# The first product of a chunked recurrent scan as one whole-array matmul for two heads instead of two half-array matmuls

## The chip, the core and the metric

The kernel runs on one core of one Trainium2 chip. A core has a matrix engine (TensorE, PE in the profile, with its weight loader PEld), a vector engine (DVE), a scalar engine (ACT), GpSimd (POOL) and a queue engine for transfers (SP). The metric is the device time of one execution in microseconds (us).

## What is computed

One block of a streaming encoder on an input of 2048 frames by 1024 channels, all in float32: a normalisation, one wide input projection, two branches, gates, an output projection, a residual and a last normalisation. The change touches the first branch, a recurrence per head (16 heads of 64 channels):

```python
def frame_step(S, inp):
    r_t, w_t, k_t, v_t, a_t, b_t = inp
    sa = jnp.einsum('bhij,bhj->bhi', S, a_t)
    S = S * w_t[:, :, None, :] + sa[..., None] * b_t[:, :, None, :] + v_t[..., None] * k_t[:, :, None, :]
    return S, jnp.einsum('bhij,bhj->bhi', S, r_t)
...
h = rms_norm(x, norm_g[l])
z = h @ w_in[l]
zs, gate_a, u, gate_b, m_a, m_b = jnp.split(z, SPLIT_POINTS, axis=-1)
...
merged = jax.nn.sigmoid(m_a) * (y_a @ p_a[l]) + jax.nn.sigmoid(m_b) * (y_b @ p_b[l])
x = x + merged @ w_out[l]
```

The second branch is a diagonal complex state-space scan (S5). The kernel does not walk frame by frame: it takes chunks of 64 frames, solves a triangular system for each chunk, and carries the 64 by 64 state of each head from chunk to chunk.

## The kernel before

**Work units.** Frames are cut into four blocks of 512 (`tb`), heads into eight pairs (`p`); a unit is a pair of heads in one block of frames, 32 in all. Each of them goes through `prep1` (elementwise work), `prep2` (products inside each chunk, the triangular solve on DVE in `solve`), `scan` and two post steps. Three units are in work at a time: while `scan` runs for one, `prep2` runs for the next and `prep1` for the one after.

**The scan.** A unit has eight chunks, so there are 256 chunks in all. Both heads of a pair lie side by side on the 128 partitions: head 0 on partitions 0 to 63, head 1 on 64 to 127 (`HS`). Of each chunk `cur` is a 128 by 128 array (tile SU): its diagonal 64 by 64 blocks hold the two heads' states, the others the chunk's values. A chunk has three slots:

- slot 1: px, the first product, with AT as weights and `cur` as the moving operand, one matmul for each head (L928); DVE copies px from PSUM (the matrix engine's output memory) to rh; ACT makes us, the decayed state (L933).
- slot 2: po gets the state's part of the output (L937); pu is the product of the solved inverse R with rh (L940); DVE and ACT scale it back into `cur` (L941, L942).
- slot 3: pn is the product that makes the next state (L946); DVE writes the next chunk's state (L954); po gets its second part (L956).

px, pn and the second part of po use 128 rows and 64 columns of the array, po's first part and pu 64 by 64.

**AT** is filled in `prep2`: products A of L819 are masked or scaled into it (L825 to L827), a piece of it goes out by DMA for the triangular solve (L832), and L906 writes its diagonal blocks at the end.

**What sets the order.** The order is written out by hand: the loop at the end of the function calls, slot by slot, one step of `scan`, one of `prep2` and so on, and then takes one or two pieces of the projections from a stream (`gm`), six matmuls of 512 columns each (L488 to L490, operands split in two parts of the type fp32r, three products). So on PE, small products of the scan stand between projection pieces. DVE's small chain of the solve is woven in by the class `Woven`, whose helper line is L75: most DVE instructions carry that line in the profile.

After the scan (about 2170 us) come the S5 branch and the output stage, which the change does not touch.

Of the kernel before, what the change touches and what calls it, by code (L numbers as in the profile page):

```python
# [10 lines left out]
F32 = mybir.dt.float32  # L11
F32R = mybir.dt.float32r
AF = mybir.ActivationFunctionType
ALU = mybir.AluOpType
# [3 lines left out]
P = 128  # L18
# [5 lines left out]
C = 64  # L24
NC = TB // C
# [28 lines left out]


class Woven:
    """An engine whose every call is followed by one call of a chain of small dependent ones."""

    def __init__(self, eng):
        self.eng, self.chain, self.due = eng, iter(()), 0  # L60
# [21 lines left out]
def tile_rwkv7_s5_block(  # L82
# [32 lines left out]
    pe, act, pool, sp = nc.tensor, nc.scalar, nc.gpsimd, nc.sync  # L115
    raw_dve = nc.vector
    dve = Woven(raw_dve)
    x = x[0]
    out = out[0]
# [26 lines left out]
    ones = wp.tile([P, 4, P], F32, tag="raw", name="ones")[:, 0, :]  # L146
# [6 lines left out]
    for i in range(2):  # L153
        for j in range(2):
            pool.affine_select(
                out=amask[64 * i:64 * i + 64, j, :], in_=amask[64 * i:64 * i + 64, j, :],
# [107 lines left out]
    if True:  # L264
        one = ph1.enter_context(tc.tile_pool(name="one", bufs=1))
        phu = ExitStack()
        u1 = phu.enter_context(tc.tile_pool(name="u1", bufs=1, side="right"))
        sm = ph1.enter_context(tc.tile_pool(name="sm", bufs=3))
# [7 lines left out]
        up = phup.enter_context(tc.tile_pool(name="up", bufs=2))  # L276
        ust = up.tile([P, NP, C], F32, tag="ust", bufs=1, name="ust")
        pool.memset(ust, 0.0)
        HS = (slice(0, 64), slice(64, 128))
# [526 lines left out]
        am = amask.rearrange("p a t -> p (a t)").unsqueeze(1)  # L806

        def prep2(p, tb):
            n = f"_{p}_{tb}"
            u = U[p, tb]  # L810
            bk, ar, v, dd = u["bk"], u["ar"], u["v"], u["dd"]
            at = up.tile([P, NC, 2, 2 * C], F32, tag="AT", name="AT" + n)
            ld = drx.tile([2, 2, NC, 32, 32], F32, tag="ld", name="ld" + n)
            for c2 in range(NC // 4):
                pas = [psm.tile([P, 4, 2 * C], F32, tag="m", name=f"A{n}_{c2}_{h}") for h in range(2)]
                for i in range(4):
                    c = 4 * c2 + i
                    for h in range(2):
                        pe.matmul(pas[h][:, i, :], bk[HS[h], c, h:h + 2, :].rearrange("p a s -> p (a s)"), ar[HS[h], c, :], start=True, stop=True)  # L819
                cs_ = slice(4 * c2, 4 * c2 + 4)  # L820
                for h in range(2):
                    o_ = HS[1 - h]
                    for i in range(4):
                        c = 4 * c2 + i
                        act.activation(out=at[HS[h], c, h, 0:C], in_=pas[h][HS[h], i, 0:C], func=AF.Copy, scale=dd[HS[h], c:c + 1])  # L825
                    dve.tensor_tensor(out=at[o_, cs_, h, 0:C], in0=pas[h][o_, :, 0:C], in1=am[o_, :, 0:C].to_broadcast([C, 4, C]), op=ALU.mult)
                    dve.tensor_tensor(out=at[:, cs_, h, C:2 * C], in0=pas[h][:, :, C:2 * C], in1=am[:, :, C:2 * C].to_broadcast([P, 4, C]), op=ALU.mult)  # L827
                if c2 == 1:
                    for h in range(2):
                        for b in range(2):  # L830
                            s0 = 64 * h + 32 * b
                            sp.dma_start(out=ld[h, b].rearrange("c s t -> s c t"), in_=at[s0:s0 + 32, :, h, 32 * b:32 * b + 32])  # L832
                yield
            ix = u1.tile([P, 32, 32], F32, tag="IX", name="IX" + n)
            ldf = ld.rearrange("h b c s t -> (h b c) s t")
# [47 lines left out]
            r64 = up.tile([P, NC, C], F32, tag="R64", name="R64" + n)  # L883
            for h in range(2):
                for b in range(2):
                    s0 = 64 * h + 32 * b
# [5 lines left out]
            t11 = u1.tile([P, NC, 32], F32, tag="TM", name="T11" + n)  # L892
# [4 lines left out]
            pz = psm.tile([P, TB], F32, tag="m", name="pz" + n)  # L897
            for c in range(NC):
                for h in range(2):
                    s0 = 64 * h  # L900
                    pe.matmul(pz[s0 + 32:s0 + 64, 32 * c:32 * c + 32], at[s0:s0 + 32, c, h, 32:64], t11[s0:s0 + 32, c, :], start=True, stop=True)
            for h in range(2):
                s0 = 64 * h + 32
                act.copy(zt[s0:s0 + 32].rearrange("p c t -> p (c t)"), pz[s0:s0 + 32, 0:256])
            for h in range(2):
                act.copy(at[HS[h], :, h, 0:C], ar[HS[h], :, 0:C])  # L906
            yield
            pr = psm.tile([P, TB], F32, tag="m", name="pr" + n)
            for c in range(NC):
                for h in range(2):  # L910
                    s0 = 64 * h
                    pe.matmul(pr[s0:s0 + 32, 32 * c:32 * c + 32], zt[s0 + 32:s0 + 64, c, :], r64[s0 + 32:s0 + 64, c, 32:64], start=True, stop=True)
            for h in range(2):
                s0 = 64 * h
# [3 lines left out]
        def scan(p, tb):  # L918
            n = f"_{p}_{tb}"
            u = U[p, tb]  # L920
            ar, at, r64, bt, decs, dd, su = (u[k] for k in ("ar", "at", "r64", "bt", "dec", "dd", "su"))
            po = u["po"] = pso.tile([P, TB], F32, tag="o", name="po" + n)
            for c in range(NC):
                dec = decs[:, c, :]
                cur = su[:, c, :]
                px = pst.tile([P, 512], F32, tag="st", name=f"px{n}_{c}")
                for h in range(2):
                    pe.matmul(px[HS[h], 0:C], at[:, c, h, 0:C], cur[:, HS[h]], start=True, stop=True)  # L928
                rh = sm.tile([P, C], F32, tag="rh", name=f"rh{n}_{c}")
                dve.tensor_copy(rh, px[:, 0:C])  # L930
                us = sm.tile([P, C], F32, tag="us", name=f"us{n}_{c}")
                for h in range(2):
                    act.activation(out=us[HS[h]], in_=cur[HS[h], HS[h]], func=AF.Copy, scale=dec[HS[h]])  # L933
                yield
                oc = po[:, c * C:(c + 1) * C]
                for h in range(2):
                    pe.matmul(oc[HS[h]], cur[HS[h], HS[h]], ar[HS[h], c, C:2 * C], start=True, stop=False)  # L937
                pu = pst.tile([P, 512], F32, tag="st", name=f"pu{n}_{c}")
                for h in range(2):
                    pe.matmul(pu[HS[h], 0:C], r64[HS[h], c, :], rh[HS[h]], start=True, stop=True)  # L940
                dve.tensor_scalar(out=cur[0:64, 0:64], in0=pu[0:64, 0:C], scalar1=dd[0:64, c:c + 1], scalar2=None, op0=ALU.mult)  # L941
                act.activation(out=cur[64:128, 64:128], in_=pu[64:128, 0:C], func=AF.Copy, scale=dd[64:128, c:c + 1])  # L942
                yield
                pn = pst.tile([P, 512], F32, tag="st", name=f"pn{n}_{c}")
                for h in range(2):
                    pe.matmul(pn[HS[h], 0:C], bt[:, c, h, :], cur[:, HS[h]], start=True, stop=True)  # L946
                for h in range(2):
                    if c + 1 < NC:
                        nxt = su[HS[h], c + 1, HS[h]]
                    elif tb % 2 == 0:  # L950
                        nxt = U[p, tb + 1]["su"][HS[h], 0, HS[h]]
                    else:
                        nxt = ust[HS[h], p, :]
                    (raw_dve if h == 0 else dve).scalar_tensor_tensor(out=nxt, in0=pn[HS[h], 0:C], scalar=dec[HS[h]], in1=us[HS[h]], op0=ALU.mult, op1=ALU.add)  # L954
                for h in range(2):
                    pe.matmul(oc[HS[h]], cur[:, HS[h]], at[:, c, h, C:2 * C], start=False, stop=True)  # L956
                yield

        MU, AD, SU = ALU.mult, ALU.add, ALU.subtract
# [543 lines left out]
        with tc.manual_schedule():  # L1503
# [13 lines left out]
            for n in range(-1, NU + 1):  # L1517
                credit = OFF if n == 0 else credit if n > NU - 2 else 0.0
                sc = scan(*units[n]) if 0 <= n < NU else none
                p2 = prep2(*units[n + 1]) if n + 1 < NU else none  # L1520
                a = units[n + 2] if n + 2 < NU else None
                b = units[n - 1] if 1 <= n else None
# [73 lines left out]
    if True:  # L1596
# [3 lines left out]
        for tb in range(NTB):  # L1600
# [44 lines left out]
            for j in range(TB // P):  # L1645
# [16 lines left out]
                for q in range(2):  # L1662
                    qs = slice(q * 512, (q + 1) * 512)
                    dve.scalar_tensor_tensor(out=sq[:, qs], in0=xt[:, qs], scalar=ss[:, 0:1], in1=fgb[:, qs], op0=ALU.mult, op1=ALU.mult)
                    if tb == NTB - 1 and j == TB // P - 1 or q:
                        o_ = qs if tb == NTB - 1 and j == TB // P - 1 else slice(0, D)
# [31 lines left out]
```

## Time and profile before

| what | value |
|---|---|
| median of 3 runs | 2781.81 us (2778.14 to 2783.49) |
| profiled execution, span from its first to its last instruction | 2782.6 us |
| mean granted TensorE clock | 0.988 |
| PE, PEld busy | 2690.9 us (97%), 1959.3 us (70%) |
| DVE, ACT, POOL busy | 1898.7 us (68%), 1372.9 us (49%), 611.4 us (22%) |
| px (L928), records on PE | 1024, from 147.0 to 2166.6 us |

For the profiled execution there is no time of its own besides its span; the span lies inside the range of the three runs. In the profile a plain f32 product appears as two passes, each with a weight load and a matmul, so the 512 px products are 1024 records. Ends of matmuls are modelled and they overlap: what a matmul costs its engine is read from the distance of starts, not from its duration.

### The profile page before, as it was taken

What the parts mean: (1) busy time and instruction counts of PE and PEld (TensorE: products, weight loads), DVE (VectorE), ACT (ScalarE), POOL (GpSimd) and SP (SyncE); (2) the same over time, 40 slices, a digit from 0 to 9 for tenths busy, and PEclk for the clock granted to TensorE, in tenths of its full rate; (3) what the DMA queues carried; (4) which work ended last, traced back from release to release, by engine and by line L of the source; (5) the groups of instructions that cost most, each with busy time, mean ns of one, the idle gap of its engine ahead of it and who ended that gap; (6) DMA issues with size and microseconds to landing.
All of it is one profiled execution on the core that took longest, in us unless ns stands there. A gap on an engine that the chain in (4) does not pass through costs nothing.

```text
span 2782.6 us, 52007 instructions
## 1 busy us (share of the span) xinstructions
PE 2690.9 (97%) x18700; PEld 1959.3 (70%) x18700; DVE 1898.7 (68%) x5620; ACT 1372.9 (49%) x3355; POOL 611.4 (22%) x985
## 2 busy tenths in 40 slices
PE   6999999999999999999999999999989999999998
PEld 4777677667777766777677777776766777777777
DVE  5656667767666787667776766667668788756544
ACT  6455554555555576555454555555554443423321
POOL 2221212122221333222212121222232200111110
PEclk9999999999999999999999999999989999999999
DMA  3222323222222443323323232322366656756533
GB/s 109 77 77 68 94 76 96 73 82 79 77 84 73 132 126 106 95 77 81 86 69 92 72 89 73 91 81 76 106 177 188 214 141 168 227 181 178 163 113 99
DMA packets 256361, 303.73 MB, mean 109 GB/s; under 512 B 159745, under 2 KB 172134, under 8 KB 255078
## 3 DMA queue, kind: packets, MB, share of 16 engines
q1 hardware_dynamic: 210502, 150.94, 20.3%
q0 software_dynamic: 45600, 149.46, 18.1%
q8 instruction: 148, 2.42, 0.4%
q14 instruction: 111, 0.91, 0.1%
HBM read 219.91 MB, written 71.70 MB: 105 GB/s over the span
## 4 chain that ended last, share of the span: by engine, by line
PE 47%; DVE 6%; DMA 4%; ACT 2%; issue 2%; SPq 0%; POOL 0%; DVEq 0%; POOLq 0%; ACTq 0%
PE pout L1656 2%; PE pout L1658 2%; PE pout L1657 2%; PE pma L488 1%; PE pga L488 1%; PE pmb L488 1%; PE px L928 1%; PE pv L488 1%; PE pk L488 1%; PE pr L488 1%; PE pn L946 1%; PE A L819 1%; PE po L937 1%; DMA sgb<-sb_d 1%; PE pma L490 1%
## 5 line engine op out<-in xcount | busy, mean ns | idle before, releaser
L942 ACT ACTIVATE SU<-pu,dd 64x64 f32<-64x64 f32 x256 | 79.2, 310 | 398.8 <-DVE SU L75 327.6
L869 DVE TENSOR_TENSOR RF<-RF,TM 128x60 f32<-128x60 f32 (+24 forms) x992 | 228.2, 230 | 28.3
L865 DVE TENSOR_TENSOR TM<-RF,IX 128x60 f32<-128x60 f32 (+24 forms) x992 | 227.4, 229 | 26.6 <-DMA IX<-ld 4.3
L933 ACT ACTIVATE us<-SU,dec 64x64 f32<-64x64 f32 x512 | 176.3, 344 | 70.4 <-DVE SU L954 62.8
L75 DVE TENSOR_TENSOR AT<-A,amask 64x256 f32<-64x256 f32 (+1 forms) x256 | 102.2, 418 | 115.9 <-ACT AT L825 110.4
L75 DVE TENSOR_SCALAR SU<-pu,dd 64x64 f32<-64x64 f32 x256 | 70.0, 274 | 162.8 <-PE pu L940 160.3
L954 DVE SCALAR_TENSOR_TENSOR SU<-pn,dec,us 64x64 f32<-64x64 f32 x240 | 65.6, 273 | 110.6 <-PE pn L946 110.1
L825 ACT ACTIVATE AT<-A,dd 64x64 f32<-64x64 f32 x512 | 116.8, 303 | 38.3 <-PE A L819 36.3
L928 PEld LDWEIGHTS px<-SU,AT 128*64 128x64 f32 x1024 | 53.9, 135 | 101.8 <-issue 50.8
L946 PEld LDWEIGHTS pn<-SU,BT 128*64 128x64 f32 x1024 | 54.3, 135 | 98.3 <-issue 40.5
L937 PEld LDWEIGHTS po<-AR,SU 64*64 64x64 f32 x1024 | 50.1, 132 | 97.0 <-issue 88.0
L488 PE MATMUL ppa<-yhi,whi_pa 128*128 128x512 f32 x256 | 115.7, 452 | 2.0 <-ACT whi_pa L224 1.1
L75 DVE COPY rh<-px 128x64 f32<-128x64 f32 x256 | 56.7, 222 | 82.0 <-PE px L928 77.2
L488 PE MATMUL pma<-hhi,whi_ma 128*128 128x512 f32 x256 | 112.7, 440 | 0.0
L488 PE MATMUL pmb<-hhi,whi_mb 128*128 128x512 f32 x256 | 112.6, 440 | 0.0
L488 PE MATMUL pk<-hhi,whi_k 128*128 128x512 f32 x256 | 112.5, 440 | 0.0
L488 PE MATMUL pga<-hhi,whi_ga 128*128 128x512 f32 x256 | 112.2, 438 | 0.0
L488 PE MATMUL pv<-hhi,whi_v 128*128 128x512 f32 x256 | 111.2, 434 | 0.3 <-ACT carry L441 0.3
L488 PE MATMUL pr<-hhi,whi_r 128*128 128x512 f32 x256 | 111.5, 435 | 0.0
L490 PE MATMUL ppa<-yhi,wlo_pa 128*128 128x512 f32 x256 | 103.9, 406 | 2.5 <-DVE wlo_pa L75 2.5
L489 PE MATMUL ppa<-ylo,whi_pa 128*128 128x512 f32 x256 | 103.5, 404 | 0.5 <-DVE ylo L75 0.5
L1656 PE MATMUL pout<-wohi,mhi 128*128 128x512 f32 x256 | 100.5, 392 | 2.9 <-ACT mhi L255 2.8
(373 smaller groups left out, 7942.5 us busy)
## 6 DMA issues: line engine op xcount, KB each, us to landing
IX<-ld SPq DMA_DIRECT2D x128, 128.0 KB
raw_pa<-in_p_a_dram POOLq DMA_DIRECT2D x64, 256.0 KB, 4.6
raw_mb<-in_w_in_dram POOLq DMA_DIRECT2D x50, 256.0 KB, 3.5
raw_r<-in_w_in_dram POOLq DMA_DIRECT2D x36, 256.0 KB, 3.7
raw_k<-in_w_in_dram POOLq DMA_DIRECT2D x36, 256.0 KB, 3.5
raw_v<-in_w_in_dram POOLq DMA_DIRECT2D x36, 256.0 KB, 3.4
raw_ga<-in_w_in_dram POOLq DMA_DIRECT2D x34, 256.0 KB, 3.5
ce<-cw SPq DMA_DIRECT2D x16, 514.0 KB
```

The costliest lines, as they stand in the source:

```text
L75: r = f(*a, **kw)
L488: pe.matmul(ps, hi[:, k, :], xhi[:, kk_, :], start=(kk_ == 0), stop=False)
L489: pe.matmul(ps, hi[:, k, :], xlo[:, kk_, :], start=False, stop=False)
L490: pe.matmul(ps, lo[:, k, :], xhi[:, kk_, :], start=False, stop=(kk_ == 7))
L825: act.activation(out=at[HS[h], c, h, 0:C], in_=pas[h][HS[h], i, 0:C], func=AF.Copy, scale=dd[HS[h], c:c + 1])
L865: raw_dve.tensor_tensor(out=tm[:, 0:na, 0:nt], in0=rf[:, 0:na, s:s + 1].to_broadcast([P, na, nt]), in1=ix[:, s:s + 1, s + 1:32].to_broadca ...
L869: raw_dve.tensor_tensor(out=rf[:, 0:na, s + 1:32], in0=rf[:, 0:na, s + 1:32], in1=tm[:, 0:na, 0:nt], op=ALU.add)
L928: pe.matmul(px[HS[h], 0:C], at[:, c, h, 0:C], cur[:, HS[h]], start=True, stop=True)
L933: act.activation(out=us[HS[h]], in_=cur[HS[h], HS[h]], func=AF.Copy, scale=dec[HS[h]])
L942: act.activation(out=cur[64:128, 64:128], in_=pu[64:128, 0:C], func=AF.Copy, scale=dd[64:128, c:c + 1])
L946: pe.matmul(pn[HS[h], 0:C], bt[:, c, h, :], cur[:, HS[h]], start=True, stop=True)
L1656: pe.matmul(ps, mhi[:, k, js], whi[:, k, qs], start=(k == 0), stop=False)
```

## The change

AT's inner layout is turned from (head, 64 columns of the first kind and 64 of the second) to (kind, head, 64 columns). Both heads' weights of the first product then lie side by side, 128 columns, and the two px matmuls become one: 128 columns of weights against all 128 columns of `cur`. Its result is 128 by 128; the two diagonal blocks are what was computed before, the other two are not used. rh becomes 128 by 128 too and is copied whole, with two buffers instead of three; pu reads its diagonal blocks. A docstring is emptied, and one line less stands before px's successors, so lines after L927 move by one.

```diff
-            at = up.tile([P, NC, 2, 2 * C], F32, tag="AT", name="AT" + n)
+            at = up.tile([P, NC, 2, 2, C], F32, tag="AT", name="AT" + n)
...
-                        act.activation(out=at[HS[h], c, h, 0:C], in_=pas[h][HS[h], i, 0:C], func=AF.Copy, scale=dd[HS[h], c:c + 1])
-                    dve.tensor_tensor(out=at[o_, cs_, h, 0:C], in0=pas[h][o_, :, 0:C], in1=am[o_, :, 0:C].to_broadcast([C, 4, C]), op=ALU.mult)
-                    dve.tensor_tensor(out=at[:, cs_, h, C:2 * C], in0=pas[h][:, :, C:2 * C], in1=am[:, :, C:2 * C].to_broadcast([P, 4, C]), op=ALU.mult)
+                        act.activation(out=at[HS[h], c, 0, h, :], in_=pas[h][HS[h], i, 0:C], func=AF.Copy, scale=dd[HS[h], c:c + 1])
+                    dve.tensor_tensor(out=at[o_, cs_, 0, h, :], in0=pas[h][o_, :, 0:C], in1=am[o_, :, 0:C].to_broadcast([C, 4, C]), op=ALU.mult)
+                    dve.tensor_tensor(out=at[:, cs_, 1, h, :], in0=pas[h][:, :, C:2 * C], in1=am[:, :, C:2 * C].to_broadcast([P, 4, C]), op=ALU.mult)
...
-                            sp.dma_start(out=ld[h, b].rearrange("c s t -> s c t"), in_=at[s0:s0 + 32, :, h, 32 * b:32 * b + 32])
+                            sp.dma_start(out=ld[h, b].rearrange("c s t -> s c t"), in_=at[s0:s0 + 32, :, 0, h, 32 * b:32 * b + 32])
...
-                for h in range(2):
-                    pe.matmul(px[HS[h], 0:C], at[:, c, h, 0:C], cur[:, HS[h]], start=True, stop=True)
-                rh = sm.tile([P, C], F32, tag="rh", name=f"rh{n}_{c}")
-                dve.tensor_copy(rh, px[:, 0:C])
+                pe.matmul(px[:, 0:P], at[:, c, 0].rearrange("p h t -> p (h t)"), cur, start=True, stop=True)
+                rh = sm.tile([P, P], F32, tag="rh", bufs=2, name=f"rh{n}_{c}")
+                dve.tensor_copy(rh, px[:, 0:P])
...
-                    pe.matmul(pu[HS[h], 0:C], r64[HS[h], c, :], rh[HS[h]], start=True, stop=True)
+                    pe.matmul(pu[HS[h], 0:C], r64[HS[h], c, :], rh[HS[h], HS[h]], start=True, stop=True)
...
-                    pe.matmul(oc[HS[h]], cur[:, HS[h]], at[:, c, h, C:2 * C], start=False, stop=True)
+                    pe.matmul(oc[HS[h]], cur[:, HS[h]], at[:, c, 1, h, :], start=False, stop=True)
```

L901 and L906 read and write AT under its new indices in the same way.

On PE, at the first chunk of the first unit (pu_0 and pu_1 are here projections of the S5 input, SU the array `cur`; at a row's end stands the size of the result), the change reads:

```order
 L489 MATMUL pu_0_1502<-hlo_172,whi_u_0_1398 128x512
 L490 MATMUL pu_0_1502<-hhi_171,wlo_u_0_1399 128x512
-L928 MATMUL px_0_0_1517<-SU_0_1103,AT_0_969 64x64 x2
+L927 MATMUL px_0_0_1517<-SU_0_1103,AT_0_969 128x128
 L488 MATMUL pu_1_1503<-hhi_402,whi_u_0_1398 128x512
 L489 MATMUL pu_1_1503<-hlo_403,whi_u_0_1398 128x512
```

Nothing moved: one px of 128 by 128 stands where two of 64 by 64 stood. 222 of the 256 chunks have a projection (L488) right behind px.

At the next chunk, on PE before the change, px stands ahead of `prep2`'s transposes of the next unit (pb, L842) and a row of sums:

```order
L490 MATMUL pu_1_1503<-hhi_402,wlo_u_1_1444 128x512
L928 MATMUL px_0_1_1657<-SU_0_1103,AT_0_969 64x64 x2
L842 MATMUL pb_1_0_1671<-ident,BK_1_1389 128x64 x8
L761 MATMUL sums_1681<-kh_1_1291,selr 32x512
L488 MATMUL pga_0_1684<-hhi_171,whi_ga_0_1531 128x512
```

and after it:

```order
L490 MATMUL pu_1_1503<-hhi_402,wlo_u_1_1444 128x512
L927 MATMUL px_0_1_1656<-SU_0_1103,AT_0_969 128x128
L842 MATMUL pb_1_0_1669<-ident,BK_1_1389 128x64 x8
L761 MATMUL sums_1679<-kh_1_1291,selr 32x512
L488 MATMUL pga_0_1682<-hhi_171,whi_ga_0_1530 128x512
```

Again only px changed. 31 chunks have L842 behind px; of the last three, two have L937 there and one L759. On DVE, the only rows that differ are the 256 copies rh, 128x128 instead of 128x64.

## Rows read from the trace of the kernel before

**Rows 1.** The page, busy time of each engine, share of the span, instructions.

```profile
PE 2690.9 (97%) x18700; PEld 1959.3 (70%) x18700; DVE 1898.7 (68%) x5620; ACT 1372.9 (49%) x3355; POOL 611.4 (22%) x985
```

**Rows 2.** Busy time by stretch: length, each engine's (instructions), clock, DMA share, GB/s.

```profile
147.00:500.00 353.00, 351.86 (x2749) 247.46 (x2749) 235.94 (x783) 182.62 (x496) 79.98 (x130) 1.00 0.30 82
...
1500.00:2000.00 500.00, 499.74 (x3949) 351.87 (x3948) 344.39 (x1133) 260.71 (x635) 111.69 (x181) 1.00 0.30 82
2000.00:2175.00 175.00, 165.03 (x1110) 116.17 (x1110) 136.25 (x511) 80.11 (x183) 54.23 (x86) 0.93 0.61 173
```

**Rows 3.** PE's waits, whole span: who waited for whom, total us, times, longest.

```profile
PE px L928 <- DVE SU L954: 6.3, 11, 1.7
...
PE pn L946 <- DVE SU L75: 2.7, 5, 0.7
...
PE pu L940 <- DVE rh L75: 1.1, 2, 0.6
```

**Rows 4.** Timeline of PE and PEld near 147 us: start, us, engine, instruction, count, [idle before].

```profile
146.41 0.39 PE L489 MATMUL pu<-hlo,whi_u 128*128 128x512 f32 x1
146.64 0.40 PE L490 MATMUL pu<-hhi,wlo_u 128*128 128x512 f32 x1
146.97 0.34 PE L928 MATMUL px<-SU,AT 128*64 128x64 f32 x4
147.24 0.50 PE L488 MATMUL pu<-hhi,whi_u 128*128 128x512 f32 x1
147.57 0.40 PE L489 MATMUL pu<-hlo,whi_u 128*128 128x512 f32 x1
...
146.97 0.20 PEld L928 LDWEIGHTS px<-SU,AT 128*64 128x64 f32 x4 [0.37 <-issue]
```

**Rows 5.** px's weight loads: group (busy, mean ns, idle before); durations, first and last start.

```profile
L928 PEld LDWEIGHTS px<-SU,AT 128*64 128x64 f32 x1024 | 53.9, 135 | 101.8 <-issue 50.8
...
L928 PEld LDWEIGHTS px<-SU,AT x1024: 132/136/227, 147.0 to 2166.6; 128*64 128x64 f32 x171
```

**Rows 6.** Timeline of PE at two plain f32 blocks on the whole array, L707 and L1308.

```profile
76.43 0.39 PE L490 MATMUL pk<-hhi,wlo_k 128*128 128x512 f32 x1
76.66 0.95 PE L707 MATMUL pss<-onec,sq 128*128 128x2 f32 x8
77.46 0.48 PE L488 MATMUL pk<-hhi,whi_k 128*128 128x512 f32 x1
77.78 0.39 PE L489 MATMUL pk<-hlo,whi_k 128*128 128x512 f32 x1
...
2244.85 0.39 PE L490 MATMUL ppa<-yhi,wlo_pa 128*128 128x512 f32 x1
2245.08 0.59 PE L1308 MATMUL px<-uR,m 128*128 128x256 f32 x2
2245.51 0.59 PE L1309 MATMUL px<-uR,m 128*128 128x256 f32 x2
2245.76 0.58 PE L488 MATMUL ppa<-yhi,whi_pa 128*128 128x512 f32 x1
2246.18 0.39 PE L489 MATMUL ppa<-ylo,whi_pa 128*128 128x512 f32 x1
```

**Rows 7.** Timeline of PE where the half-height transposes L842 follow px.

```profile
158.84 0.40 PE L490 MATMUL pu<-hhi,wlo_u 128*128 128x512 f32 x1
159.16 0.34 PE L928 MATMUL px<-SU,AT 128*64 128x64 f32 x4
159.43 0.71 PE L842 MATMUL pb<-ident,BK 64*128 64x64 f32 x8
```

**Rows 8.** Two groups of DVE: result and source, count, busy us, mean ns, idle before.

```profile
L75 DVE COPY rh<-px 128x64 f32<-128x64 f32 x256 | 56.7, 222 | 82.0 <-PE px L928 77.2
...
L75 DVE TENSOR_TENSOR AT<-A,amask 128x256 f32<-128x256 f32 x128 | 53.1, 415 | 0.9
```

**Rows 9.** Tile rh: what its instructions waited for, us and times.

```profile
PE px L928: 77.2, 73
DVE rh L75: 2.8, 6
```

More of the change, by code (lines that the diff above doesn't have):

```diff
@@ L900, in prep2 @@
                     s0 = 64 * h
-                    pe.matmul(pz[s0 + 32:s0 + 64, 32 * c:32 * c + 32], at[s0:s0 + 32, c, h, 32:64], t11[s0:s0 + 32, c, :], start=True, stop=True)
+                    pe.matmul(pz[s0 + 32:s0 + 64, 32 * c:32 * c + 32], at[s0:s0 + 32, c, 0, h, 32:64], t11[s0:s0 + 32, c, :], start=True, stop=True)
             for h in range(2):
@@ L905, in prep2 @@
             for h in range(2):
-                act.copy(at[HS[h], :, h, 0:C], ar[HS[h], :, 0:C])
+                act.copy(at[HS[h], :, 0, h, :], ar[HS[h], :, 0:C])
             yield
```

## The prediction

> **What bounds the kernel now.** I began with the busy times of the whole span [rows 1]: PE, the matrix engine, is busy 97% of it, DVE 68%, ACT 49%. Since busy matmuls overlap, that alone proves little, so I read the stretches next [rows 2]. The recurrent scan, which the change touches, runs from 147 to about 2167 us. From 147 to 500 PE is busy 351.86 of 353 us and from 1500 to 2000 499.74 of 500, at a granted clock of 1.00 (the 2.4 GHz level), while DVE stands at 0.67 and 0.69 of the time. The third view is the list of PE's waits [rows 3]: over the whole run the scan's first product px waited 6.3 us for DVE, the product pu behind it 1.1 us, pn 2.7 us. PE is nearly never kept waiting there, so PE's own stream of instructions sets the end, and a change is worth what it takes out of, or puts into, that stream.
>
> The fourth view is the order in time on PE around one px [rows 4]. Projection matmuls of 512 columns follow each other every 0.23 us (146.41 to 146.64). After the one at 146.64, px starts only at 146.97, 0.33 us later, so 0.10 us late. Its four passes (two heads, each f32 product run as two passes) keep the array until the weights of the next projection start at 147.24. That projection's own successor starts at 147.57, again 0.33 us on, another 0.10 us lost. From 146.64 to 147.57 are 0.93 us; two undisturbed steps would be 0.46. **One px block therefore costs 0.46 us** (to the rounding of the rows): 0.10 to get in, 0.26 for four half-array passes, 0.10 to get out. The weight loader's row says the same from its side: it idled 0.37 us before px. That is no single event: over all px it idled 101.8 us [rows 5], 0.40 us for each of 256 blocks.
>
> **The change part by part.** It removes 256 of 512 px matmuls, that is 512 of 1024 passes, and makes each that is left twice as wide: 128 columns of weights and 128 moving ones instead of 64 and 64.
>
> *Getting in and out.* Two blocks of plain f32 products on the whole array show what a block without a change of shape does [rows 6]. L707's first pass starts 0.23 us after the projection before it (76.43 to 76.66), the ordinary step. L1308 does the same (2244.85 to 2245.08). Both are f32 and both wait on other engines' results, as px does, so neither the number format nor a semaphore makes the 0.10 us; the half-array shape is what px has and they don't. I take both 0.10 us as gone.
>
> *The two wide passes.* No row shows a pass with 128 columns of weights and 128 moving ones of f32. From the side of the weights: L707 has 128 columns of weights and 2 moving ones; its eight passes take 77.78 − 76.43 − 0.46 = 0.89 us, 0.11 each. From the side of the moving columns: L1308 and L1309 have 256; their four passes take 2246.18 − 2244.85 − 0.46 = 0.87, 0.22 each, so 128 would take 0.11. If loading the second pass's weights lies beside the first pass's streaming, two passes are 0.22 us; if load and streaming follow each other, 0.44 us. In L1308 a load of 128 columns (0.11 by L707) hides entirely behind streaming, so I take 0.22 and keep 0.44 for the range. Nothing excludes a little more than that, so the block's gain lies between 0.24 us and nothing.
>
> A rule of the Trainium skill speaks against the change here: the page TensorEngine Tiling (Array Packing), section Theoretical Speedup, gives up to twofold throughput when operands of 64 or fewer columns use two tiles of the array at once. By that rule the four half passes would cost only half of the whole array's 0.22, an estimated 0.11 us, and merging them would lose 0.11 us × 256 = 28 us. The trace does not agree with it: the half passes take 0.26.
>
> *How often.* In the program's order 222 of the 256 px are followed by a whole-array projection; for these the block falls from 0.46 to 0.22, **222 × 0.24 = 53 us**. 31 are followed by the half-height transposes of L842, which change the shape anyway; there px takes 159.43 − 159.16 = 0.27 us up to L842 [rows 7], and two wide passes 0.22, so 31 × 0.05 = 1.5 us. The other three I leave at nothing. On PE that is 55 us.
>
> *What DVE gets.* The copy rh now takes 128 × 128 out of PSUM. 128 × 64 takes 222 ns, a 128 × 256 product with the mask, also out of PSUM, 415 ns [rows 8]: 1.0 ns per column, so the copy grows by some 64 ns, 256 × 0.064 = 16 us on DVE. Its cover is DVE's idle third in the scan. If that cover were gone, all 16 us could reach the end.
>
> *What waits.* Behind rh comes pu, one projection piece later. The copy is 0.06 us longer and PE reaches pu 0.24 us sooner, so 0.30 us of pu's margin is spent. Six of the 256 pu blocks wait for rh today, 2.8 us of the weight loader's time [rows 9]; 73 of the copies started when px ended, the others later, because DVE had other work. No grouped view gives the margin of each. I let one block in ten lose its whole gain: 26 × 0.24 = 6 us, rounded with the rest to **5 us given back**. The later steps (SU, pn, the next state) keep their distances, and px's wait on both heads' states is the one that it had for its second head. In the stretch from 2000 us, DVE is at 0.78 and PE already waits [rows 2]; px come every (2166.6 − 147.0)/255 = 7.9 us [rows 5], some 20 of them there, so 5 us more may be lost. I keep that for the range.
>
> *At nothing:* the order inside AT moves addresses only, with runs of 64 numbers for the engines and 32 for the DMA as before; rh's two buffers instead of three are enough, because rh of a chunk is read before the next chunk's is written; PE also waits for 87 more of its own earlier results, all at least 24 matmuls back, hence past. The final product reads the same 64 columns.
>
> **Sum:** −55 + 5 = −50 us against the profiled execution's span of 2782.6: 2732.6. The median of the runs, 2781.8, is 0.8 us below that span, so I predict 2732.
>
> **The rivals.** (a) *The wait moves to DVE.* With PE quicker and rh longer, pu and the later steps wait for DVE in many chunks, and between a third and four fifths of the 50 us come back: 2745 to 2770. For it: pu's margin shrinks by 0.30 us in every chunk. Against it: PE's waits in the scan are a few us in all [rows 3], DVE has a third of the time free.
>
> (b) *The wide passes run in series, or the gaps stay.* At 0.44 us per block the gain is 0.02 × 222 = 4 us; if instead the 0.10 us on both sides belong to the wait for the state and not to the shape, the block is 0.42, the gain 0.04 × 222 = 9 us. 2773 to 2778. Against it: both whole-array blocks of rows 6.
>
> (c) *Slower: the half passes ran side by side, and merged they run one after the other.* At twice 0.26 the two wide passes would take 0.52 us. Even without the gaps the block then costs 0.06 × 222 + 0.25 × 31 = 21 us more: 2803. It decides from 0.46 us per block upward. Against it: whole-array passes of twice the columns take 0.22, and of as many weights 0.11. By the Trainium skill's tiling rule above, a loss of 28 us would be 2810. No run of before can show it for this very shape.
>
> (d) *The change does not do what it says.* Excluded: the built order has one px row of 128 by 128 for each pair, and no other row changes places.
>
> **How the numbers follow.** The forecast (2724 to 2742) has 0.70; a little more gain than that, if px's few waits shrink too, 0.02; (a) 0.15; (b) 0.08, half of it within the bound; (c) 0.05. A measurement of this kernel can tell about 0.2%, 5.6 us, from no change. Faster by more: 0.70 + 0.02 + 0.15 + 0.04 = 0.91; within it 0.04; slower 0.05. The range runs from 2716, as if nothing were given back and px's waits went as well, to 2760, which takes in the DVE stretch's 5 us, the copy's 16 us and the better half of (a); outside lie the rest of (a), (b) and (c), somewhat under 0.2.
>
> **What would show it.** Right: px as two passes of 128 columns, the first 0.23 us after the projection before it, the block at about 0.22 us over two steps; the loader's idle time before px falling from 101.8 us to some 15; rh near 286 ns; the scan's last px at about 2117 us instead of 2167, and the tail as long as before. For (a): pu's waits for rh in the tens of us. For (b): the block near 0.42. For (c): two px passes 0.26 us apart. Wrong altogether: a scan as long as before with PE waiting, or a tail that grows.

## The result, and the profile after

The changed kernel takes 2737.79 us (median of 4 runs, 2736.08 to 2739.66), the kernel before on the same chip 2781.33 us (4 runs): a ratio of 0.9846, 95% interval 0.9832 to 0.9860. It is 43.5 us faster; the forecast was 2732, about 50 us faster, and the range held the time.

The page's first part, of the changed kernel (busy time, share of the span, instructions; it answers to [rows 1]):

```profile
PE 2638.4 (96%) x18188; PEld 1985.9 (73%) x18188; DVE 1913.0 (70%) x5620; ACT 1372.1 (50%) x3355; POOL 612.3 (22%) x985
```

512 passes are gone from PE, and PE is busy 52.5 us less, yet the span fell by only 44.6 us, from 2782.6 to 2738.0. The same stretches as in [rows 2]:

```profile
147.00:500.00 353.00, 350.38 (x2712) 258.28 (x2712) 245.86 (x808) 187.74 (x506) 80.69 (x131) 1.00 0.31 83
...
1500.00:2000.00 500.00, 495.21 (x3940) 365.61 (x3940) 357.42 (x1136) 274.90 (x668) 118.38 (x193) 1.00 0.32 90
2000.00:2175.00 175.00, 161.31 (x936) 118.19 (x937) 137.90 (x480) 76.97 (x184) 52.51 (x82) 0.95 0.65 194
```

Where PE had been busy 499.74 of 500 us, it now is 495.21, with DVE at 0.71 of the time instead of 0.69, and the granted clock as before. PE has begun to wait. For what, its list of waits tells (total us, times, longest), beside [rows 3]:

```profile
PE px L927 <- DVE SU L75: 14.6, 15, 3.7
...
PE pn L945 <- DVE SU L75: 3.7, 7, 0.8
...
PE pu L939 <- DVE rh L75: 2.9, 6, 0.9
```

All three grew: px from 6.3, pn from 2.7, pu from 1.1. The timeline of PE and of its weight loader at the first px (start, us) answers to [rows 4]:

```profile
145.20 0.39 PE L490 MATMUL pu<-hhi,wlo_u 128*128 128x512 f32 x1
145.43 0.38 PE L927 MATMUL px<-SU,AT 128*128 128x128 f32 x2
145.57 0.48 PE L488 MATMUL pu<-hhi,whi_u 128*128 128x512 f32 x1
145.89 0.39 PE L489 MATMUL pu<-hlo,whi_u 128*128 128x512 f32 x1
...
145.20 0.42 PEld L927 LDWEIGHTS px<-SU,AT 128*128 128x128 f32 x2
```

px now starts 0.23 us behind the projection, the ordinary step, and its weights are loaded beside that projection, from 145.20. From 145.20 to 145.89 are 0.69 us. Two undisturbed steps take 0.47 us together (0.234 each, in the median of this trace), which leaves a block of 0.22 us, where it was 0.46. The loader's idle time before px and px's first and last start, beside [rows 5]:

```profile
L927 PEld LDWEIGHTS px<-SU,AT 128*128 128x128 f32 x512 | 95.1, 190 | 42.7 <-DVE SU L75 22.6
...
L927 PEld LDWEIGHTS px<-SU,AT x512: 186/189/333, 145.2 to 2124.1; 128*128 128x128 f32 x171
```

The idle time fell from 101.8 us to 42.7, not to the 15 that I had named; 22.6 us of what is left is waiting for the state (SU). From the first px to the last are 1978.9 us instead of 2019.6: **40.7 us of the 44.6 come from the scan**; px starts 1.8 us sooner and the tail is 2.1 us shorter, both within what two executions differ by. The last px comes at 2124 us and not at the 2117 that I had named.

Where L842 follows, beside [rows 7]:

```profile
157.16 0.39 PE L490 MATMUL pu<-hhi,wlo_u 128*128 128x512 f32 x1
157.39 0.38 PE L927 MATMUL px<-SU,AT 128*128 128x128 f32 x2
157.70 0.71 PE L842 MATMUL pb<-ident,BK 64*128 64x64 f32 x8
```

From the projection to L842 it is 0.54 us instead of 0.59, the 0.05 that the prediction had. The copy, and what tile rh waited for, beside [rows 8, 9]:

```profile
L75 DVE COPY rh<-px 128x128 f32<-128x128 f32 x256 | 73.9, 289 | 75.3 <-PE px L927 71.1
...
DVE rh L75: 7.7, 17
```

289 ns instead of 222 (286 were expected), and pu's block waits for rh 17 times instead of 6, 7.7 us instead of 2.8.

**The balance of PE's stream.** I summed the distance of each matmul's start from the one ahead of it, by kind, from the first px to the last. px and the projections together became 49.3 us shorter, pu's part 3.7 us longer, pn's 3.5, the rest 1.1: 41.0 us. Against the 55 us expected on PE, 14 came back: some 6 in px and the projections, the others in pu, pn and the rest. Within the first sum px itself gave some back. Its ordinary start is 0.33 us after the instruction ahead of it before the change and 0.23 after it; the starts later than that add up to 7.0 us over the 256 px before, and to 17.6 us after it. These 10.6 us more are not all loss: at the place shown next, a late px of four passes held PE for 0.58 us up to the next projection, a late one of two passes holds it for 0.24.

**Where px waits.** Of these 17.6 us, 13.0 fall on the fifth chunk of a unit, in 17 of 32 units. Here is such a place, the timeline around the fifth chunk of unit 4, first the three engines of the changed kernel:

```profile
418.75 0.24 DVE L869 TENSOR_TENSOR RF<-RF,TM 128x76 f32<-128x76 f32 x1
419.02 1.81 DVE L865 TENSOR_TENSOR TM<-RF,IX 128x72 f32<-128x72 f32 x1
420.86 0.23 DVE L869 TENSOR_TENSOR RF<-RF,TM 128x72 f32<-128x72 f32 x1
421.02 0.27 DVE L953 SCALAR_TENSOR_TENSOR SU<-pn,dec,us 64x64 f32<-64x64 f32 x1
421.32 0.29 DVE L75 SCALAR_TENSOR_TENSOR SU<-pn,dec,us 64x64 f32<-64x64 f32 x1
...
419.43 1.29 POOL L788 TENSOR_TENSOR rkb<-rkb,zv 128x512 f32<-128x512 f32 x1
...
418.48 0.34 PE L945 MATMUL pn<-SU,BT 128*64 128x64 f32 x4
...
421.66 0.49 PE L927 MATMUL px<-SU,AT 128*128 128x128 f32 x2 [1.13 <-DVE SU L75]
```

and DVE and PE at the same place of the kernel before:

```profile
426.89 1.82 DVE L865 TENSOR_TENSOR TM<-RF,IX 128x72 f32<-128x72 f32 x1
...
428.90 0.27 DVE L954 SCALAR_TENSOR_TENSOR SU<-pn,dec,us 64x64 f32<-64x64 f32 x1
...
426.60 0.34 PE L946 MATMUL pn<-SU,BT 128*64 128x64 f32 x4
...
429.23 0.65 PE L928 MATMUL px<-SU,AT 128*64 128x64 f32 x4 [0.57 <-DVE SU L954]
```

pn is done in good time, but the two DVE instructions that make the next state stand behind a step of the solve that takes 1.81 us where its neighbours take 0.23, while POOL multiplies 128 by 512 numbers (L788). That was so before. But PE had used more time up to there, and waited 0.57 us; now it arrives sooner and waits 1.13. So of what the chunks ahead of it saved in this unit, 0.56 us went into the wait.

### The profile page after: what moved, and what is told of

It reads as the page before. It is cut to its first block, busy times and chain, and to the rows that moved or that the text cites. A ratio compares the mean times of both kernels' runs of the same rounds, so it can differ in the third digit from the quotient of the medians.

```text
span 2738.0 us, 50952 instructions
## 1 busy us (share of the span) xinstructions
PE 2638.4 (96%) x18188; PEld 1985.9 (73%) x18188; DVE 1913.0 (70%) x5620; ACT 1372.1 (50%) x3355; POOL 612.3 (22%) x985
## 5 line engine op out<-in xcount | busy, mean ns | idle before, releaser
L75 DVE COPY rh<-px 128x128 f32<-128x128 f32 x256 | 73.9, 289 | 75.3 <-PE px L927 71.1
L927 PEld LDWEIGHTS px<-SU,AT 128*128 128x128 f32 x512 | 95.1, 190 | 42.7 <-DVE SU L75 22.6
L488 PE MATMUL ppa<-yhi,whi_pa 128*128 128x512 f32 x256 | 114.5, 447 | 2.0 <-ACT whi_pa L224 1.2
L927 PE MATMUL px<-SU,AT 128*128 128x128 f32 x512 | 100.8, 279 | 14.7 <-DVE SU L75 14.6
L488 PE MATMUL pmb<-hhi,whi_mb 128*128 128x512 f32 x256 | 112.5, 439 | 0.0
L488 PE MATMUL pma<-hhi,whi_ma 128*128 128x512 f32 x256 | 112.1, 438 | 0.0
L488 PE MATMUL pk<-hhi,whi_k 128*128 128x512 f32 x256 | 111.6, 436 | 0.0
L488 PE MATMUL pga<-hhi,whi_ga 128*128 128x512 f32 x256 | 111.5, 436 | 0.0
L488 PE MATMUL pr<-hhi,whi_r 128*128 128x512 f32 x256 | 111.1, 434 | 0.0
L488 PE MATMUL pv<-hhi,whi_v 128*128 128x512 f32 x256 | 110.6, 432 | 0.3 <-ACT carry L441 0.3
```

Of the source, the lines that this page charges most:

```text
L75: r = f(*a, **kw)
L488: pe.matmul(ps, hi[:, k, :], xhi[:, kk_, :], start=(kk_ == 0), stop=False)
L927: pe.matmul(px[:, 0:P], at[:, c, 0].rearrange("p h t -> p (h t)"), cur, start=True, stop=True)
```

## Theories

A: the gain is the shape of px on the array, 0.10 us on each side, and the passes cost what [rows 6] told. B: the part that is missing (55 us expected on PE, 41 in the scan) was given back by the longer copy. C: it was given back where DVE stands still beside POOL, copy or not.

## Experiments: what the gain is

**Only AT's new inner order** (`e1_layout`).

```diff
-                pe.matmul(px[:, 0:P], at[:, c, 0].rearrange("p h t -> p (h t)"), cur, start=True, stop=True)
-                rh = sm.tile([P, P], F32, tag="rh", bufs=2, name=f"rh{n}_{c}")
-                dve.tensor_copy(rh, px[:, 0:P])
+                for h in range(2):
+                    pe.matmul(px[HS[h], 0:C], at[:, c, 0, h, :], cur[:, HS[h]], start=True, stop=True)
+                rh = sm.tile([P, C], F32, tag="rh", name=f"rh{n}_{c}")
+                dve.tensor_copy(rh, px[:, 0:C])
...
-                    pe.matmul(pu[HS[h], 0:C], r64[HS[h], c, :], rh[HS[h], HS[h]], start=True, stop=True)
+                    pe.matmul(pu[HS[h], 0:C], r64[HS[h], c, :], rh[HS[h]], start=True, stop=True)
```

> Only AT's new inner order; px is two half-array matmuls again and rh a 128 by 64 copy. Theory A (the gain is the shape of px on the array): as before, 2781 us, within 3. Rival (the gain comes from the order inside AT): near the changed kernel, 2738.

Measured: 2782.87 us, before 2782.51 in the same session; ratio 1.0003 (0.9993 to 1.0012). The order inside AT is worth nothing.

**Two whole-array matmuls for each px** (`e2_two_wide`).

```diff
-                pe.matmul(px[:, 0:P], at[:, c, 0].rearrange("p h t -> p (h t)"), cur, start=True, stop=True)
+                for h in range(2):
+                    pe.matmul(px[:, HS[h]], at[:, c, 0].rearrange("p h t -> p (h t)"), cur[:, HS[h]], start=True, stop=True)
```

> The changed kernel with px as two matmuls of 128 weight columns, each with one head's 64 moving columns: four whole-array passes, same results and same copy. Theory A (the 0.10 us on each side belong to the half-array shape): px starts 0.23 us after the projection before it, four passes of 0.11 make a block of 0.44 us, 0.02 less than before; with the longer copy the kernel is at 2781 to 2790. Rival (the 0.10 us belong to px's wait for the state): the gaps stay, block 0.64 us, 0.18 more than before on some 222 px, 2820 or above.

Measured: 2786.27 us against 2782.51, ratio 1.0007 (0.9998 to 1.0016). The timeline of PE at the first px:

```profile
145.58 0.39 PE L490 MATMUL pu<-hhi,wlo_u 128*128 128x512 f32 x1
145.81 0.55 PE L928 MATMUL px<-SU,AT 128*128 128x64 f32 x4
146.17 0.48 PE L488 MATMUL pu<-hhi,whi_u 128*128 128x512 f32 x1
146.49 0.39 PE L489 MATMUL pu<-hlo,whi_u 128*128 128x512 f32 x1
```

px waits for the same state as ever and yet starts after 0.23 us: the 0.10 us on each side are the shape's. 146.49 − 145.58 − 0.47 is a block of 0.44 us, four passes of 0.11. So both halves of the sum are shown one by one: the gaps go, and the number of whole-array passes decides what is left.

The Trainium skill says both things on one page, TensorEngine Tiling (Array Packing): a change of tiling mode drains the engine (Tiling Modes), which these rows agree with, and operands of 64 or fewer columns gain up to twofold by tiles (Theoretical Speedup). As far as these rows reach they agree with that too: the two products kept apart take 0.44 us as four whole-array passes (of 128 weight columns each) and took 0.26 as four half-array ones, 1.7 times less. But getting in and out took 0.20 us of that back, and one merged product, 0.22 us, beats both.

**The kernel before with the long copy** (`e3_long_copy`).

```diff
-                rh = sm.tile([P, C], F32, tag="rh", name=f"rh{n}_{c}")
-                dve.tensor_copy(rh, px[:, 0:C])
+                rh = sm.tile([P, 2, C], F32, tag="rh", bufs=2, name=f"rh{n}_{c}")
+                dve.tensor_copy(rh, px[:, 0:C].unsqueeze(1).to_broadcast([P, 2, C]))
...
-                    pe.matmul(pu[HS[h], 0:C], r64[HS[h], c, :], rh[HS[h]], start=True, stop=True)
+                    pe.matmul(pu[HS[h], 0:C], r64[HS[h], c, :], rh[HS[h], h, :], start=True, stop=True)
```

> The kernel before with rh copied as 128 by 128 (the same 64 columns twice), px unchanged. It prices the copy alone, 0.066 us more for each of 256. Theory B (DVE's extra 17 us are what gave back part of the gain): 2790 to 2798. Theory C (the extra lies in DVE's free time and only counts where DVE is behind, in one chunk of eight): 2782 to 2788.

Measured: 2782.54 us against 2782.51, ratio 1.0000 (0.9989 to 1.0011), the copy at 289 ns. In the kernel before, 17 us more on DVE cost nothing that these runs can tell. Theory B falls there; whether it falls in the changed kernel, where DVE has less margin, the next run asks.

**Half the moving columns** (`e7_half_moving`): head 1's first product is left out.

```diff
-                pe.matmul(px[:, 0:P], at[:, c, 0].rearrange("p h t -> p (h t)"), cur, start=True, stop=True)
-                rh = sm.tile([P, P], F32, tag="rh", bufs=2, name=f"rh{n}_{c}")
-                dve.tensor_copy(rh, px[:, 0:P])
+                pe.matmul(px[:, 0:C], at[:, c, 0].rearrange("p h t -> p (h t)"), cur[:, 0:C], start=True, stop=True)
+                rh = sm.tile([P, C], F32, tag="rh", name=f"rh{n}_{c}")
+                dve.tensor_copy(rh, px[:, 0:C])
...
-                    pe.matmul(pu[HS[h], 0:C], r64[HS[h], c, :], rh[HS[h], HS[h]], start=True, stop=True)
+                    pe.matmul(pu[HS[h], 0:C], r64[HS[h], c, :], rh[HS[h]], start=True, stop=True)
```

> The changed kernel with only head 0's 64 moving columns in px (128 columns of weights, one matmul of two passes) and rh a 128 by 64 copy; head 1's first product is left out. If the two wide passes are bound by their weights at 0.11 us each, the block stays at 0.22 us and only the copy gets short again. Theory B (the copy gave back the missing part): some 10 us below the changed kernel, 2728. Theory C (the missing part is DVE standing still in one chunk of eight, copy or not): 2733 to 2737. If moving columns count beside weights, the block falls below 0.2 and the kernel below 2725.

Measured: 2739.26 us (2732.26 to 2741.89), as the changed kernel's 2737.79, above what either theory had. At its first px:

```profile
146.79 0.39 PE L490 MATMUL pu<-hhi,wlo_u 128*128 128x512 f32 x1
147.02 0.33 PE L927 MATMUL px<-SU,AT 128*128 128x64 f32 x2
...
147.47 0.40 PE L489 MATMUL pu<-hlo,whi_u 128*128 128x512 f32 x1
```

147.47 − 146.79 − 0.47 = 0.21: half the moving columns save next to nothing, so the passes are bound by their 128 columns of weights. The short copy did take px's late starts down from 17.6 to 10.5 us, but the time did not follow beyond what runs differ by: the scan, first to last px, was 3.5 us shorter, while three executions with px as it was before (before, `e1_layout`, `e3_long_copy`) differ by 3.8. So in the changed kernel the copy uses up DVE's margin in the fifth chunk. The 10 us of theory B did not come; a few us are not excluded.

## Experiments: where the rest went

**rkb times v on DVE, in the changed kernel and in the one before** (`e4_rkv_dve`, `e5_rkv_dve_before`), the same line in both:

```diff
-                pool.tensor_tensor(out=rkv_, in0=rkb, in1=U[a]["v"], op=ALU.mult)
+                dve.tensor_tensor(out=rkv_, in0=rkb, in1=U[a]["v"], op=ALU.mult)
```

> The changed kernel with one product of 128 by 512 (rkb times v, L788, once a unit) on DVE instead of POOL. While it ran on POOL, one DVE instruction of the solve beside it took 1.81 us instead of 0.22, and px of the fifth chunk of a unit then waited for DVE. Theory C (that stall gave back the missing part): px's excess over its ordinary start falls from 17.6 us towards 5, the kernel to 2724 to 2731. Rival (DVE is simply full in that chunk, whoever multiplies): 2736 to 2742.

> The same move of rkb times v to DVE in the kernel before. Theory C: the stall costs less there, since PE reaches the fifth px later (px's excess is 7.0 us): 2775 to 2780, so that the distance to the changed kernel with the same move is near the 55 us of the bare sum on PE. Rival: 2780 to 2785, distance as now, 43 us.

Measured: 2725.58 us for the changed kernel (ratio to before 0.9801, 0.9786 to 0.9817), 2771.98 for the one before (0.9967, 0.9956 to 0.9979; below both ranges stated for it), before itself 2782.09. The same place, fifth chunk of unit 4, in the changed kernel with the move, DVE and PE:

```profile
420.28 0.23 DVE L865 TENSOR_TENSOR TM<-RF,IX 128x72 f32<-128x72 f32 x1
420.55 0.23 DVE L869 TENSOR_TENSOR RF<-RF,TM 128x72 f32<-128x72 f32 x1
420.70 0.27 DVE L953 SCALAR_TENSOR_TENSOR SU<-pn,dec,us 64x64 f32<-64x64 f32 x1
421.01 0.29 DVE L75 SCALAR_TENSOR_TENSOR SU<-pn,dec,us 64x64 f32<-64x64 f32 x1
421.33 0.23 DVE L865 TENSOR_TENSOR TM<-RF,IX 128x68 f32<-128x68 f32 x1
421.47 0.68 DVE L75 TENSOR_TENSOR rkb<-rkb,zv 128x512 f32<-128x512 f32 x1
...
421.63 0.38 PE L927 MATMUL px<-SU,AT 128*128 128x128 f32 x2
```

The very instruction that took 1.81 us takes 0.23, and px starts without a wait. In the kernel before and in the changed one, 31 steps of the solve took over 1 us (48 us in all); with the move none does, in either, and DVE pays for the products, 32 in all, 0.68 us each, 22 us. px's late starts fall from 17.6 to 3.7 us in the changed kernel and from 7.0 to 3.4 in the one before. So theory C holds for px. But it says less about the difference of the two than I expected: between these two kernels the distance is 46.4 us, not near 55. In PE's stream px and the projections are now 55.1 us shorter, the whole bare sum; pu's part is 4.2 us longer, pn's 2.5, the rest 4.2, and the scan 44.2 us shorter. By the intervals 46.4 is not told apart from 43.5.

**Unit by unit.** I took the time from one unit's first px to the next unit's, before minus after. The bare sum is 7 × 0.24 + 0.05 = 1.73 us for each unit. With the move on both sides, the 26 units 0 to 12 and 16 to 28 (counted from 0) gain 42.9 of 45 us, but the six units 13 to 15 and 29 to 31 only 1.3 of 10. Without the move the 26 gain 38.1 and the six 2.9. So the stall beside POOL took about 5 us of the gain, and 7 to 9 us are missing in six units, stall or not. Units 29 to 31 hold the stretch from 2000 us; their first and last px, before:

```profile
1972.74 0.34 PE L928 MATMUL px<-SU,AT 128*64 128x64 f32 x4
...
2166.58 0.34 PE L928 MATMUL px<-SU,AT 128*64 128x64 f32 x4
```

and after:

```profile
1931.27 0.38 PE L927 MATMUL px<-SU,AT 128*128 128x128 f32 x2
...
2124.05 0.38 PE L927 MATMUL px<-SU,AT 128*128 128x128 f32 x2
```

That is 193.84 us and 192.78 us, 1.1 us gained where the bare sum gives 5. From 2000 us on, px waited 5.3 us for DVE instead of 2.3. The sizes in the six units are rough: three executions with px as it was before (before, `e1_layout`, `e3_long_copy`) differ by 2.1 us in units 13 to 15 and by 2.4 in 29 to 31, in the 26 others by 0.3. What takes the gain in these six units was not tested.

**pn merged too** (`e6_pn_wide`).

```diff
-                for h in range(2):
-                    pe.matmul(pn[HS[h], 0:C], bt[:, c, h, :], cur[:, HS[h]], start=True, stop=True)
+                pe.matmul(pn[:, 0:P], bt[:, c].rearrange("p h t -> p (h t)"), cur, start=True, stop=True)
...
-                    (raw_dve if h == 0 else dve).scalar_tensor_tensor(out=nxt, in0=pn[HS[h], 0:C], scalar=dec[HS[h]], in1=us[HS[h]], op0=ALU.mult, op1=ALU.add)
+                    (raw_dve if h == 0 else dve).scalar_tensor_tensor(out=nxt, in0=pn[HS[h], HS[h]], scalar=dec[HS[h]], in1=us[HS[h]], op0=ALU.mult, op1=ALU.add)
```

> The changed kernel with pn merged in the same way (128 weight columns, 128 moving), while po's second part behind it stays two half-array matmuls. Theory A (what counts is how often the shape changes): there is still one change in and one out, the four half passes of pn that ran close behind others are replaced by two of 0.11, so the block goes from 0.58 to 0.65 to 0.70 and the kernel to 2755 to 2770. Rival (a wide pass is cheaper than the half passes it replaces): below 2738.

Measured: 2766.47 us (before 2782.09), 29 us slower than the changed kernel. The third slot's block with pn merged, PE:

```profile
171.07 0.39 PE L490 MATMUL pga<-hhi,wlo_ga 128*128 128x512 f32 x1
171.29 0.38 PE L944 MATMUL pn<-SU,BT 128*128 128x128 f32 x2
171.61 0.34 PE L954 MATMUL po<-AT,SU 128*64 128x64 f32 x4
...
172.21 0.40 PE L489 MATMUL pga<-hlo,whi_ga 128*128 128x512 f32 x1
```

172.21 − 171.07 − 0.47 = 0.67 us. The same slot of the changed kernel, with both in halves:

```profile
169.84 0.40 PE L490 MATMUL pga<-hhi,wlo_ga 128*128 128x512 f32 x1
170.17 0.34 PE L945 MATMUL pn<-SU,BT 128*64 128x64 f32 x4
170.33 0.29 PE L955 MATMUL po<-AT,SU 128*64 128x64 f32 x4
...
170.89 0.40 PE L489 MATMUL pga<-hlo,whi_ga 128*128 128x512 f32 x1
```

170.89 − 169.84 − 0.47 = 0.58 us. The change of shape did not go away, it moved between pn and po, and merging alone costs. The same edit that paid at px, a lone small product between whole-array work, loses at pn.

**po's second part deferred** (`e8_deferred`): on top of pn merged.

```diff
+                if c:
+                    for h in range(2):
+                        pe.matmul(oc[HS[h]], su[:, c - 1, HS[h]], at[:, c - 1, 1, h, :], start=False, stop=True)
                 oc = po[:, c * C:(c + 1) * C]
...
-                for h in range(2):
-                    pe.matmul(oc[HS[h]], cur[:, HS[h]], at[:, c, 1, h, :], start=False, stop=True)
+                if c == NC - 1:
+                    for h in range(2):
+                        pe.matmul(oc[HS[h]], cur[:, HS[h]], at[:, c, 1, h, :], start=False, stop=True)
```

> As the kernel with pn merged, but po's second part of a chunk is issued in the next chunk's second slot, ahead of po's first part and pu, which are tiles anyway (the last chunk of a unit keeps its place). Theory A: pn then stands among whole-array matmuls, its block falls from 0.58 to 0.22, the second slot's grows from 0.57 by 0.13 to 0.20: 0.16 to 0.23 us for 224 chunks, 36 to 51 us, of which a third may be given back to DVE: 2695 to 2715. Rival (no more to be had, DVE is the bound): 2730 or above.

Measured: 2747.91 us, a miss on the slow side, in the rival's range: 10 us slower than the changed kernel. pn's block is 0.22 as expected, but the second slot's grew from 0.57 to 0.84, more than the 0.20 allowed, and the waits grew:

```profile
PE px L927 <- DVE SU L75: 18.9, 19, 3.0
...
PE pn L947 <- ACT SU L944: 11.8, 22, 1.9
```

px's late starts were 22.1 us here. And a merged pn waits for the later of its two producers, ACT's half of SU, where in halves head 0 could go first: a wait that the changed kernel does not have among its costly ones. By the blocks alone this kernel would still have gained; px's and pn's waits together are 12 us more than in the changed kernel, and the rest of the miss is not accounted for.

**The deferral with rkb times v on DVE** (`e9_deferred_rkv`), the edit of `e4_rkv_dve` on top of the last.

> The kernel with pn merged and po's second part deferred, with rkb times v on DVE as well. If the stall beside POOL is what px waited for there (22 us of excess), it falls by some 14 to 18 us to 2730 to 2734. It would still not beat the changed kernel with that move alone (2725.6), because the merged pn waits for the later of its two producers, ACT's half of SU (11.8 us of PE's time, about 0.1 us in the mean over its blocks), where the two half products let head 0 go first. Rival (the deferral pays once DVE keeps up): below 2715.

Measured: 2725.58 us (ratio 0.9804, 0.9785 to 0.9822). It gained 22 us, more than expected, px's late starts at 5.5 us, but pn still waits 9.7 us for ACT, and it is no better than the changed kernel with that move alone (2725.58 as well).

**Both large products of POOL on DVE** (`e10_both_dve`): as `e4_rkv_dve`, and

```diff
-            pool.tensor_tensor(out=ar[:, :, C:2 * C], in0=c3(r), in1=c3(eg), op=ALU.mult)
+            dve.tensor_tensor(out=ar[:, :, C:2 * C], in0=c3(r), in1=c3(eg), op=ALU.mult)
```

> The changed kernel with rkb times v and also the other large product on POOL (AR from zr and eG, L730, 1.30 us, 32 times) on DVE. Beside L730, DVE instructions are longer by 13 us in all, and on DVE it costs 32 times 0.68 = 22 us. If only a stall at a place where DVE is behind counts, no change: 2722 to 2730. Rival (every POOL product of this size costs PE time): 2715 or below.

Measured: 2722.22 us (2720.55 to 2724.63; ratio 0.9789, 0.9773 to 0.9805), the fastest kernel of this study, 58 us under before. It lies in the first theory's range, and its interval overlaps that of `e4_rkv_dve`: that the second product helped is not shown.

## Why the prediction was right, and by how much it missed

- *PE sets the end, and a change is worth what it takes out of PE's stream.* Right: 40.7 of 44.6 us came from the scan; the tail stayed, and so did the mean granted clock (0.988 before, 0.991 after).
- *The 0.10 us on each side go.* Right, by the timeline after and by `e2_two_wide`, where the product stays in two and the gaps go all the same.
- *Two wide passes, 0.22 us, weights beside streaming.* Right: block 0.22. That the weights bind them is shown by `e7_half_moving`.
- *55 us on PE.* Right: 55.1 us in px and the projections, where px's late starts are equal on both sides (`e4_rkv_dve` against `e5_rkv_dve_before`).
- *5 us given back.* **This term was too small: the scan gave back 14.** I counted pu's margin (expected up to 6, measured 3.7 us) and wrote that the later steps keep their distances and that px's wait is the one that it had. That was the step that failed: px's late starts grew by 10.6 us and pn's part by 3.5. What a chunk saves does not all stay saved: in unit 4 the fifth px waits 0.56 us longer for a state that DVE finishes hardly sooner; counted from the unit's first px, the fifth starts only 0.13 us earlier than before. Of the 14 us about half are missing in 26 units, most of that by the stall beside POOL, and half in units 13 to 15 and 29 to 31, for a cause that stays open. The 5 us that I kept for the range for the stretch from 2000 us were needed: units 29 to 31 gave back some 4.
- *The copy's 16 us on DVE.* 17 us in the profile. In the kernel before they cost nothing (`e3_long_copy`), as the cover said; in the changed kernel they lengthened px's waits, with no cost that the runs can tell (`e7_half_moving`).
- *The Trainium skill's tiling rule.* The prediction set the four half passes against the one merged product and found the trace at odds with the rule. That compared unlike things: the rule is on the same small products with and without tiles, and there, by `e2_two_wide`, 0.44 us against 0.26 agrees with it. So the 0.11 us and the loss of 28 us did not follow from the rule; the sum did not use them.
- *Rivals.* (b), the series or the staying gaps, and (c), the halves side by side, are excluded by the block. (a), the wait that moves to DVE, happened in part: of the 50 us forecast 6.5 came back, an eighth instead of a third or more, and pu's waits for rh stayed at 7.7 us.

## What to carry to other kernels

A small product alone among whole-array matmuls pays for entering and leaving another shape. Here that was 0.20 of 0.46 us, and computing twice as much on the whole array was cheaper. It pays only where the change of shape disappears: merging pn, whose neighbour stayed in halves, cost 29 us, and a merged product waits for the later of its inputs. What PE saves can be lost at the next place where another engine is behind. Here 26 of 32 units kept 38 of 45 us and the other six 3 of 10, so the gain has to be looked for unit by unit; DVE's average idle third did not tell it.

## What the runs showed of the hardware

A DVE product of two SBUF operands took 1.81 us instead of 0.23 while POOL multiplied 128 by 512 numbers (1.29 us), and 31 such long steps, 30 of them overlapping that product in the trace, went away when the product moved to DVE at 0.68 us each: 12 us off the changed kernel, 10 off the one before. The Trainium skill's SBUF — State Buffer page, section Who interferes with whom, says that a DVE instruction with two SBUF inputs contends with a GpSimd instruction that reads SBUF. These rows agree. I had not looked for it, because POOL was busy only 22% of the time and the waits that I read named DVE.

The three small f32 shapes cost alike by pass on the whole array: 128 weight columns with 2, 64 or 128 moving columns took 0.11 us.
